# An mLSTM stage reordered: gate columns and decay rows between chunks, key and query pieces in pairs, the head norm in halves

## The chip, the cores and the metric

The kernel runs on one core of one Trainium2 chip. That core has a matrix engine (TensorE, PE in the profile, with its weight loads as PEld), a vector engine (VectorE, DVE), a scalar engine (ScalarE, ACT), a general-purpose engine (GpSimd, POOL), and a queue that issues DMA transfers (SyncE, SP). The engines run at the same time; each takes its own instructions in a fixed order and waits for others through semaphores. The large on-chip memory is SBUF. TensorE writes its results to a second, small memory, PSUM, which has eight banks of 512 float32 values per partition.

The metric is the device time of one execution in microseconds (us), lower being better.

## The reference

A decoder trunk of two layers works on 256 tokens of width 1024, in float32. Each layer is a half-step SwiGLU feed-forward, a token mixing, and another half-step feed-forward, each followed by a residual and a layer norm. The token mixer of layer 1 is the mLSTM, beside a cross-attention of 4 heads into 256 memory tokens; both read one input projection and go into one output projection. What matters here:

```python
def mlstm_mixer(u, b_gates, qk_conv_w, head_norm_g):
    b, s, _ = u.shape
    qk, v, o_pre, gates = jnp.split(u, [2 * D_TOK, 3 * D_TOK, 4 * D_TOK], -1)
    qk = jax.nn.silu(causal_dwconv(qk, qk_conv_w))
    q, k = jnp.split(qk, 2, -1)
    gates = gates.astype(jnp.float32) + b_gates.astype(jnp.float32)
    log_i = gates[..., :ML_HEADS]
    log_f = jax.nn.log_sigmoid(gates[..., ML_HEADS:])
    h = mlstm_chunkwise(q, k, v, log_i, log_f)
    mu = jnp.mean(h, -1, keepdims=True)
    var = jnp.mean(jnp.square(h - mu), -1, keepdims=True)
    h = (h - mu) * lax.rsqrt(var + LN_EPS) * head_norm_g.astype(jnp.float32)
    return jax.nn.sigmoid(o_pre) * h.reshape(b, s, D_TOK).astype(u.dtype)
```

There are 4 mLSTM heads of 192 columns (768 together). The reference steps through chunks of 64 tokens; the kernel computes the same as one masked product over all 256 tokens: scores of queries and keys, weighted by a decay that comes from running sums and maxima of the gates, times the values, divided by the larger of a denominator and an exponential. The convolution is causal over 4 positions, per channel.

## The kernel before

**Precision.** A float32 operand is split into two parts, a rounded one and the rest (`split`, L98: a copy on ScalarE at L99, a difference on VectorE at L100). A product is three products of parts. Where the weights are the stationary operand (`mmw`, L179), the activation's two parts lie side by side, 512 wide: L181 multiplies both by the weight's first part, L182 the first 256 by its second, and `comb` (L184) adds the bank's two halves, with a copy on ScalarE (L186) and an addition on VectorE (L187). Where the activation is stationary, `mm3` (L171) makes the three products at L175 to L177.

**Weights.** `pieces` lists all weights in the order of use, 1 MB each at most. `trace_piece` loads one into one of 3 raw buffers and splits it into one of 5 buffers; `get` asks for one piece ahead of the one that it hands out. In the mLSTM stage two of the raw buffers are lent out: one to the head norm's gains, one to the decay weights.

**Order.** The program is written in Python in a wished order, with pools of buffers; a scheduler then fixes each engine's order, and may put later work that it takes to be ready ahead of earlier work that it takes to wait. Banks of PSUM come from two pools of four, `y` (`ybank`) and `mm` (`mbank`).

**The mLSTM stage** (`mlstm_mixer`, L540), for layer 1: the output gate and the gates (L545 to L564); the query of the cross-attention (`Xattn`, tile `xq`); `gate_rows` (L574), a chain over ScalarE, VectorE and GpSimd on 4 rows, one per head; the values of heads 0 and 1 (`values(0, t)`, L697) and the cross-attention's scores (L429) in turn; `columns` (L603), which turns the gate rows into columns; `decay` (L612) twice, for two heads each, which share one bank; then six pieces of keys and queries (`qk_piece`, L627): keys 0, 1, 2 and then queries 0, 1, 2, each 256 columns in two chunks of 128, with the cross-attention's `values` (L455) between the first ones. A piece's chunk has a bank of its own; `comb` copies it to SBUF, where the convolution reads it, a scaled copy on ScalarE (L637) and three multiply-adds on VectorE (L639), and a Silu on ScalarE ends the piece (L643).

Then come the values of heads 2 and 3, with the scores of all four heads (`mscores`, L648) between them, then `numer` (L661) for the two tiles of 128 tokens: products of scores and values (L673), the division, and the norm of four heads, whose reciprocal root runs on GpSimd (`rstd_of`, L202). `tokens` (L708) multiplies by the gate (L712), transposes (L715) and splits the result into the operand `mix`. `OutProj` (L477) multiplies by the output weights in four quarters `q` of the contraction (tile `yo`): `head` does quarter 0 for both tiles, `rest` the others tile by tile, with quarter 1 of both column halves first; after each half of the columns comes the layer norm's first part (`ln_half`, L211). Tile 0's norm and transposes end under tile 1's products; the next feed-forward begins with products of tile 0 (tile `gx`).

`OutProj` and `Xattn` serve the convolution mixer of layer 0 as well.

## Time and profile before

| | |
|---|---|
| median of 3 runs | 1000.24 us (1000.14 to 1000.39) |
| span of the profiled execution, first to last instruction | 1004.1 us |
| TensorE busy, whole span | 986.8 us (98%) |
| VectorE busy, whole span | 664.8 us (66%) |
| ScalarE busy, whole span | 530.1 us (53%) |
| GpSimd busy, whole span | 39.4 us (4%) |
| TensorE busy from 704.00 to 782.65 us (query to the last head's product) | 77.87 of 78.65 us, mean granted clock 0.91 |
| TensorE busy from 782.65 to 809.60 us (output projection) | 24.98 of 26.95 us, clock 1.00 |

The profiled execution's own time is known as its span alone; it is 3.9 us longer than the median of the runs. Times in the profile count from its first instruction. A row of a stretch has its start and end, its length, the busy time of each engine with the number of instructions, the granted share of TensorE's clock, the mean busy share of the DMA engines and their GB/s. A row of the order in time has start, duration, engine, line, operation, what it writes and reads, and in square brackets how long the engine had been idle and what ended that.

### The profile page before, as it was taken

To read this page: it belongs to the slowest core of one execution; us is meant where nothing else is said; L and a number is where in the kernel's file an instruction comes from. 1 tells how busy PE (TensorE), PEld (TensorE's weight loads), DVE (VectorE), ACT (ScalarE), POOL (GpSimd) and SP (SyncE) were. 2 spreads that over 40 slices of the span, in tenths; PEclk is the share of its full clock that TensorE was granted. 3 is DMA by queue.
4 is the path that set the end of the run, shared out by engine and by line. 5 is a ranking of instruction groups with operands and counts; after the bars stand their busy time and mean duration, and the time that the engine had idled before them with its cause. 6 is when DMAs were issued, how large, how long until landed. Compare 5 with 4: busy or idle time off the path is not lost.

```text
span 1004.1 us, 12980 instructions
## 1 busy us (share of the span) xinstructions
PE 986.8 (98%) x5116; PEld 834.7 (83%) x5116; DVE 664.8 (66%) x1010; ACT 530.1 (53%) x851; POOL 39.4 (4%) x52
## 2 busy tenths in 40 slices
PE   8999999999999999999999999999999999999996
PEld 7888888888888888888788888889788788888885
DVE  6685657868677656565866656576478887556555
ACT  6565555447445545556355555535676346454540
POOL 0000000100000000000100000002300110000001
PEclk9999999999999999999999999999799999999999
DMA  8884546455535654644464646434145466546421
GB/s 277 311 295 166 210 168 212 171 228 205 187 130 187 241 201 159 218 155 180 173 246 168 215 162 213 154 111 154 78 149 205 185 236 230 199 158 216 161 84 43
DMA packets 29293, 186.90 MB, mean 186 GB/s; under 512 B 3632, under 2 KB 4656, under 8 KB 8368
## 3 DMA queue, kind: packets, MB, share of 16 engines
q1 hardware_dynamic: 29232, 186.07, 51.7%
q8 instruction: 40, 0.66, 0.2%
q14 instruction: 21, 0.17, 0.1%
HBM read 185.01 MB, written 1.05 MB: 185 GB/s over the span
## 4 chain that ended last, share of the span: by engine, by line
PE 89%; DVE 4%; POOL 2%; DMA 2%; issue 2%; ACT 0%; SPq 0%; POOLq 0%; DVEq 0%; ACTq 0%
PE gu L181 28%; PE gu L182 14%; PE y L177 8%; PE y L175 8%; PE y L176 8%; PE qkp L181 3%; PE gx L175 2%; PE gx L177 2%; PE gx L176 2%; DVE wl L100 1%; PE qkp L182 1%; PE cx L181 1%; PE cg L181 1%; PE cb L181 1%; PE yo L177 1%
## 5 line engine op out<-in xcount | busy, mean ns | idle before, releaser
L100 DVE TENSOR_TENSOR wl<-raw,wh 128x1024 fp32r<-128x1024 f32 (+1 forms) x342 | 400.6, 1195 | 147.6 <-ACT wh L99 146.8
L181 PE MATMUL gu<-x,wh 128*128 128x512 f32 x1216 | 431.1, 399 | 1.4 <-DVE s L187 1.1
L99 ACT ACTIVATE wh<-raw 128x1024 fp32r<-128x1024 f32 (+1 forms) x342 | 338.3, 1032 | 113.4 <-PE y L177 45.0
L182 PE MATMUL gu<-x,wl 128*128 128x256 f32 x1216 | 340.8, 281 | 0.4 <-DVE wl L100 0.2
L181 PEld LDWEIGHTS gu<-x,wh 128*128 128x128 f32 x1216 | 228.5, 188 | 57.4 <-DVE s L187 1.4
L182 PEld LDWEIGHTS gu<-x,wl 128*128 128x128 f32 x1216 | 230.0, 189 | 2.6 <-DVE wl L100 1.0
L175 PE MATMUL y<-wh,h 128*128 128x512 f32 x352 | 138.1, 392 | 0.0
L177 PE MATMUL y<-wh,h 128*128 128x512 f32 x352 | 137.7, 391 | 0.0
L176 PE MATMUL y<-wl,h 128*128 128x512 f32 x352 | 137.2, 390 | 0.0
L187 DVE TENSOR_TENSOR s<-s,gu 128x256 f32<-128x256 f32 x152 | 63.2, 417 | 107.6 <-ACT s L186 107.6
L186 ACT ACTIVATE s<-gu 128x256 f32<-128x256 f32 x152 | 57.4, 379 | 111.4 <-PE gu L182 110.7
L177 PEld LDWEIGHTS y<-wh,h 128*128 128x128 f32 x352 | 66.1, 188 | 14.5
L175 PEld LDWEIGHTS y<-wh,h 128*128 128x128 f32 x352 | 66.1, 188 | 14.0
L176 PEld LDWEIGHTS y<-wl,h 128*128 128x128 f32 x352 | 66.1, 188 | 13.0
L301 ACT ACTIVATE h<-s 128x256 fp32r<-128x256 f32 x76 | 31.7, 417 | 68.2 <-DVE s L298 68.0
L297 ACT ACTIVATE s<-s 128x256 f32<-128x256 f32 x76 | 31.6, 416 | 37.0 <-DVE s L187 37.0
L302 DVE TENSOR_TENSOR h<-s,h 128x256 fp32r<-128x256 f32 x76 | 32.0, 421 | 17.9 <-ACT h L301 17.9
L181 PE MATMUL qkp<-x,wh 128*128 128x512 f32 x96 | 38.6, 438 | 0.0
L175 PE MATMUL gx<-wh,x 128*128 128x512 f32 x96 | 38.2, 398 | 0.2 <-DVE x L261 0.2
L177 PE MATMUL gx<-wh,x 128*128 128x512 f32 x96 | 37.5, 391 | 0.0
L176 PE MATMUL gx<-wl,x 128*128 128x512 f32 x96 | 37.4, 390 | 0.0
L260 ACT ACTIVATE x<-xt 128x512 fp32r<-128x512 f32 x20 | 11.4, 596 | 44.2 <-PE xt L239 43.8
(191 smaller groups left out, 996.1 us busy)
## 6 DMA issues: line engine op xcount, KB each, us to landing
raw<-in_wgu SPq DMA_DIRECT2D x83, 1024.0 KB, 4.8
raw<-in_wd SPq DMA_DIRECT2D x43, 1024.0 KB, 4.8
raw<-in_wconv SPq DMA_DIRECT2D x10, 1024.0 KB, 4.8
raw<-in_wout SPq DMA_DIRECT2D x8, 1024.0 KB, 4.8
raw<-in_wm SPq DMA_DIRECT2D x7, 1024.0 KB, 4.7
gb<-in_lngb SPq DMA_DIRECT2D x6, 1024.0 KB, 4.9
raw<-in_wkv SPq DMA_DIRECT2D x4, 1024.0 KB, 4.9
raw<-in_wop SPq DMA_DIRECT2D x4, 776.0 KB, 4.2
```

Of the source, the lines that this page charges most:

```text
L99: act.activation(h, raw, AF.Copy)
L100: dve.tensor_sub(l, raw, h.bitcast(F32))
L175: pe.matmul(o, ah, bh, start=start, stop=False)
L176: pe.matmul(o, ah, bl, start=False, stop=False)
L177: pe.matmul(o, al, bh, start=False, stop=stop)
L181: pe.matmul(bank, w[0], a.rearrange("p c t -> p (c t)"), start=start, stop=False)
L182: pe.matmul(bank[:, :T], w[1], a[:, 0], start=False, stop=stop)
L186: act.activation(o, bank[:, T:], AF.Copy)
L187: dve.tensor_add(o, o, bank[:, :T])
L297: act.activation(t_[:, :256], t_[:, :256], AF.Silu)
L301: act.activation(hh, t_[:, 256:], AF.Copy)
L302: dve.tensor_sub(hT[g][:, 1, fc, :], t_[:, 256:], hh.bitcast(F32))
```

## The change

Layer 1's mLSTM stage is written in another order, and some of its steps are cut differently.

- The pieces of keys and queries come in pairs, key 0, query 0, key 1, query 1, key 2, query 2, and their weights stream in that order.
- `proj_direct` replaces `proj_ws` for them. Both chunks of a piece lie in the two halves of one bank; each step of the contraction is three 256-wide products into the same place, so that no addition of halves is needed. The convolution reads PSUM directly. Between the two chunks a function `mid` may put other work: `gate_rows` between the chunks of the cross-attention's query, `columns`, `decay(2)`, the cross-attention's transposes (`turn`) and values, one head of `mscores`, and one `numer`.
- `qk_piece` returns its Silu, which the caller places: those of key 0 and query 0 stand after the second `decay`.
- `Xattn.values` is cut in two; `turn` has all transposes and copies.
- `numer(t, a)` does one pair of heads, with a norm and a reciprocal root of its own, and the multiplication by the gate. Heads 0 and 1 of both tiles come before and within the last query piece; `tokens(t, h)` likewise does one half.
- `OutProj.head(q)` can be called for quarter 1 as well; `rest` does the quarters that are left, half by half of the columns. In layer 0 quarter 1 is thus no longer done ahead for both halves.

Comments and docstrings are dropped, which changes nothing.

```diff
-    order = [("wm", 0), ("wv", 0, 0), ("wv", 0, 1)] + [("wm", i) for i in range(1, 7)]
+    order = [("wm", 0), ("wv", 0, 0), ("wv", 0, 1)] + [("wm", i) for i in (1, 4, 2, 5, 3, 6)]
...
+    def proj_direct(w, name, use, mid=None):
+
+        b = mbank(name)
         for c in range(2):
+            if c and mid:
+                mid()
+            o = b[:, c * T:(c + 1) * T]
+            for k in range(KC):
+                s = slice(k * 256 + c * P, k * 256 + (c + 1) * P)
+                a = cur["x"][:, k]
+                pe.matmul(o, w[0][:, s], a[:, 0], start=k == 0, stop=False)
+                pe.matmul(o, w[0][:, s], a[:, 1], start=False, stop=False)
+                pe.matmul(o, w[1][:, s], a[:, 0], start=False, stop=k == KC - 1)
+            use(c, o)
...
-        def values(self, c):
-            ob = ybank(f"xo{self.l}_{c}")
+        def turn(self, c):
             for e in range(2):
                 n = f"{self.l}_{c}{e}"
-                p = self.p.pop((c, e))
+                p = self.p[c, e]
...
-        def head(self):
-            self.ws[0] = get("wo", self.l, 0)
+        def head(self, q=0):
+            self.ws[q] = get("wo", self.l, q)
             for t in range(2):
-                self.part(0, t, (0, 1))
+                self.part(q, t, (0, 1))
 
         def rest(self, gb):
-            for q in range(1, 4):
+            first = len(self.ws)
+            for q in range(first, 4):
                 self.ws[q] = get("wo", self.l, q)
             nx = new_act(f"x{self.i}")
 
             def tail(t):
-                self.part(1, t, (0, 1))
                 for h in range(2):
-                    for q in range(2, 4):
+                    for q in range(first, 4):
                         self.part(q, t, (h,))
...
-        def qk_piece(n):
-            which = 1 if n < 3 else 0
-            i = n % 3
-            r = tmp(f"qr{n}")
-            ut = tmp(f"qu{n}")
+        def qk_piece(which, i, mid=None):
+            r = tmp(f"qr{which}{i}")
 
             def use(c, b):
                 o = c * 256
-                comb(ut[:, o:o + 256], b)
                 w = [qcw[:, 6 * which + 2 * i + c, q:q + 1] for q in range(4)]
-                act.activation(r[:, o:o + 256], ut[:, o:o + 256], AF.Copy, scale=w[3])
+                act.activation(r[:, o:o + 256], b, AF.Copy, scale=w[3])
                 for q, sh in ((0, 3), (1, 2), (2, 1)):
-                    dve.scalar_tensor_tensor(r[:, o + sh:o + 256], ut[:, o:o + 256 - sh], w[q],
+                    dve.scalar_tensor_tensor(r[:, o + sh:o + 256], b[:, :256 - sh], w[q],
                                              r[:, o + sh:o + 256], op0=ALU.mult, op1=ALU.add)
...
-        xa = Xattn(1, get("wm", 0), mix)
-        gate_rows()
+        xa = Xattn(1, get("wm", 0), mix, gate_rows)
         values(0, 0)
         xa.scores(0)
         values(0, 1)
         xa.scores(1)
-        columns()
+        silu = [qk_piece(1, 0, columns)]
         decay(0)
-        decay(2)
-        qk_piece(0)
-        xa.values(0)
-        qk_piece(1)
+        silu.append(qk_piece(0, 0, lambda: decay(2)))
+        for f_ in silu:
+            f_()
+        qk_piece(1, 1, lambda: xa.turn(0))()
+        mscores(0)
+        qk_piece(0, 1, lambda: xa.values(0))()
+        xa.turn(1)
+        qk_piece(1, 2, lambda: mscores(1))()
         xa.values(1)
-        qk_piece(2)
-        qk_piece(3)
-        qk_piece(4)
-        qk_piece(5)
+        numer(0, 0)
+        qk_piece(0, 2, lambda: numer(1, 0))()
         values(1, 0)
-        mscores(0)
-        mscores(1)
-        values(1, 1)
         mscores(2)
         mscores(3)
-        numer(0)
-        numer(1)
+        values(1, 1)
+        tokens(0, 0)
+        numer(0, 1)
+        numer(1, 1)
+        tokens(1, 0)
         o = OutProj(1, mix, i)
-        tokens(0)
-        o.head()
-        tokens(1)
+        o.head(0)
+        tokens(0, 1)
+        o.head(1)
+        tokens(1, 1)
         o.rest(load_ln(i))
```

More of the change, by code (lines that the diff above doesn't have):

```diff
@@ L402, in mem_kv, with proj_ws @@
                 act.activation(kvs[l][1][:, c], b[:, l * 256:(l + 1) * 256], AF.Copy)
-    def proj_ws(w, name, use):
+    def proj_direct(w, name, use, mid=None):
+        b = mbank(name)
         for c in range(2):
+            if c and mid:
[8 more added lines that the diff above has]
+            use(c, o)
+    def proj_ws(w, name, use, mid=None):
+        for c in range(2):
+            if c and mid:
+                mid()
             b = mbank(f"{name}_{c}")
@@ L416, in trunk, with __init__ @@
     class Xattn:
-        def __init__(self, l, w, mix):
+        def __init__(self, l, w, mix, mid=None):
             self.l, self.mix = l, mix
@@ L465, in values @@
                 act.activation(p, tb, AF.Copy)
+        def values(self, c):
+            ob = ybank(f"xo{self.l}_{c}")
+            for e in range(2):
+                p = self.p.pop((c, e))
                 h0 = (2 * c + e) * 64
@@ new lines, in mlstm_mixer, with numer @@
+        hts = {}
+        def numer(t, a):
+            if a == 0:
+                hts[t] = zp.tile([P, DTOK], F32, tag="z", name=f"ht{t}")
+            ht = hts[t]
+            n = f"{t}{a}"
+            r = sp.tile([P, 2], F32, tag="dn", name="dn" + n)
+            st = sp.tile([P, 2, 6], F32, tag="hst", name="hst" + n)
+            mv = sp.tile([P, 2, 2], F32, tag="hmv", name="hmv" + n)
+            b = mbank("num" + n)
+            bv = b[:, :386].rearrange("p (a e) -> p a e", a=2)
+            for c in range(2):
+                h = 2 * a + c
+                for s in range(t + 1):
+                    lhs = E[h][:, 256:384] if s == 1 else E[h][:, tsl(t)]
+                    pe.matmul(bv[:, c, :], lhs, v1[s][:, h, :], start=s == 0, stop=s == t)
+            dve.tensor_copy(r, bv[:, :, DH])
+            dve.scalar_tensor_tensor(r, r, -1.0, r, op0=ALU.mult, op1=ALU.max)
+            dve.tensor_tensor(r, r, ecol[:, t, 2 * a:2 * a + 2], op=ALU.max)
+            dve.reciprocal(r, r)
+            dve.tensor_tensor(ht[:, 384 * a:384 * a + 384].rearrange("p (a e) -> p a e", a=2),
+                              bv[:, :, :DH], r[:, :, None].to_broadcast([P, 2, DH]), op=ALU.mult)
+            for c in range(2):
+                h = 2 * a + c
+                dve.bn_stats(st[:, c, :], ht[:, DH * h:DH * h + DH])
+                dve.bn_aggr(mv[:, c, :], st[:, c, :])
+            rs = rstd_of(mv[:, :, 1], 2, "hn" + n)
+            for c in range(2):
+                s = slice(DH * (2 * a + c), DH * (2 * a + c) + DH)
+                dve.tensor_scalar(ht[:, s], ht[:, s], mv[:, c, 0:1], rs[:, c:c + 1],
@@ L706, in values, with tokens @@
                            AF.Copy)
-        def tokens(t):
-            og = ogs[t]
-            for h in range(2):
-                s = slice(384 * h, 384 * h + 384)
-                dve.tensor_mul(og[:, s], og[:, s], hn[t][:, s])
-                b = mbank(f"tk{t}{h}")
-                for c in range(3):
-                    pe.transpose(b[:, c * P:(c + 1) * P], og[:, (3 * h + c) * P:(3 * h + c + 1) * P],
-                                 ident)
-                to_parts(mix, 3 * h, 3, t, b)
-        xa = Xattn(1, get("wm", 0), mix)
-        gate_rows()
+        def tokens(t, h):
+            b = mbank(f"tk{t}{h}")
+            for c in range(3):
+                pe.transpose(b[:, c * P:(c + 1) * P], ogs[t][:, (3 * h + c) * P:(3 * h + c + 1) * P],
+                             ident)
+            to_parts(mix, 3 * h, 3, t, b)
+        xa = Xattn(1, get("wm", 0), mix, gate_rows)
         values(0, 0)
@@ L771, in scores, with values @@
         xa.scores(1)
-    conv_mixer(mix, [scores, lambda: xa.values(0), lambda: xa.values(1)])
+    def values(c):
+        xa.turn(c)
+        xa.values(c)
+    conv_mixer(mix, [scores, lambda: values(0), lambda: values(1)])
     o = OutProj(0, mix, 1)
```

37 lines of the change are left out of this document (5 added, 32 removed).

## The prediction

> **What bounds the kernel now.** I read the page for the span, a table of stretches for the stage that the change touches, the order of single instructions on TensorE (PE) around each loss, and the groups of the pieces.
>
> ```profile
> span 1004.1 us, 12980 instructions
> PE 986.8 (98%) x5116; PEld 834.7 (83%) x5116; DVE 664.8 (66%) x1010; ACT 530.1 (53%) x851; POOL 39.4 (4%) x52
> ```
>
> TensorE is busy for 98% of the span, so time can only come from work removed there, from its idle stretches, or from its clock. The stretches (us, then busy time of each engine, then the granted clock):
>
> ```profile
> core 0: us, PE busy (x) PEld busy (x) DVE busy (x) ACT busy (x) POOL busy (x), PEclk, DMA share, GB/s
> 713.69:717.10 3.41, 2.63 (x16) 1.59 (x15) 3.09 (x9) 2.42 (x9) 1.95 (x3) 1.00 0.00 0
> 717.34:730.99 13.65, 13.65 (x38) 9.57 (x37) 8.69 (x24) 8.04 (x25) 0.00 (x0) 0.50 0.00 0
> 731.00:767.50 36.50, 36.50 (x219) 31.76 (x219) 31.04 (x59) 27.98 (x48) 0.00 (x0) 1.00 0.49 163
> 704.00:782.65 78.65, 77.87 (x407) 64.10 (x405) 55.52 (x115) 52.28 (x100) 7.72 (x10) 0.91 0.38 134
> 782.65:809.60 26.95, 24.98 (x118) 19.91 (x118) 24.13 (x59) 9.58 (x13) 6.47 (x6) 1.00 0.60 230
> ```
>
> Three losses stand there. The second row is the largest: TensorE is busy throughout 13.65 us, but with half its clock. The row above is the stretch before: 3.41 - 2.63 = 0.78 us idle, and much of the busy time on narrow operands. The last row, the output projection, has 26.95 - 24.98 = 1.97 us idle. The pieces after 731 us run with no idle time at all.
>
> What TensorE did around the drop, and how far a step of a piece is from the next, before and after the clock came back:
>
> ```profile
> 713.82 0.70 PE L434 MATMUL sc<-kT,xqT 64*128 64x256 f32 x2
> 714.97 1.13 PE L434 MATMUL sc<-kT,xqT 64*128 64x256 f32 x6 [0.45 <-ACT p L446]
> 716.02 0.22 PE L606 MATMUL cols<-ident,rows 4*128 4x4 f32 x1
> 716.58 0.22 PE L607 MATMUL cols<-ident,rows 4*128 4x4 f32 x1 [0.34 <-POOL rows L598]
> ...
> 716.79 1.52 PE L616 MATMUL negm<-rows,ident 4*128 4x256 f32 x4
> ...
> 719.05 0.63 PE L181 MATMUL qkp<-x,wh 128*128 128x512 f32 x1
> 719.69 0.63 PE L181 MATMUL qkp<-x,wh 128*128 128x512 f32 x1
> ...
> 723.02 1.22 PE L616 MATMUL negm<-rows,ident 4*128 4x256 f32 x2
> ...
> 735.94 0.40 PE L181 MATMUL qkp<-x,wh 128*128 128x512 f32 x1
> 736.18 0.28 PE L182 MATMUL qkp<-x,wl 128*128 128x256 f32 x1
> 736.30 0.40 PE L181 MATMUL qkp<-x,wh 128*128 128x512 f32 x1
> ```
>
> The last scores, the gate columns and the decay rows use 64 or 4 rows of the array and wait for ScalarE (ACT) and GpSimd (POOL); right after them the clock is halved. A step of a piece then takes 719.69 - 719.05 = 0.64 us instead of 736.30 - 735.94 = 0.36.
>
> **The change, part by part.** *Clock.* Both chunks of the first key piece, dense work, now stand on either side of the columns, and the next piece's on either side of the second decay pair. No stretch as long as that of 713.69 to 717.10 is left with narrow work and waits alone. What this is worth: at least the first piece's 2 x 8 steps, 16 x 0.28 = 4.5 us; at most half of the stretch, 6.8 us. The stretch also holds decay matmuls, slowed as well, so I take a value near the top, 6.3.
>
> [...]
>
> *Idle time before the columns.* The GpSimd chain ends only just before 716.58; with a chunk of a piece ahead of the columns they are done in time. Of the 0.78 us I take all, bounds 0 and 0.8, since the dense chunk (8 x 0.36 = 2.9 us) is longer than both waits.
>
> *The pieces themselves.* A step was a 512-wide and a 256-wide matmul; it becomes three 256-wide ones into one place of the bank, the same 768 columns. The row at 736.18 is a 256-wide one, and the next starts 0.12 us later with its weights loaded: 3 x 0.12 = 0.36, as now. Cost nothing; bounds -0.01 and +0.02 a step, 96 steps, so -1 to +2 us. What goes is the addition of the bank's halves:
>
> ```profile
> L100 DVE TENSOR_TENSOR wl<-raw,wh 128x1024 fp32r<-128x1024 f32 x12 | 14.6, 1219 | 1.8 <-ACT wh L99 1.7
> L99 ACT ACTIVATE wh<-raw 128x1024 fp32r<-128x1024 f32 x12 | 12.6, 1057 | 0.6 <-DMA raw<-in_wm 0.6
> L637 ACT ACTIVATE qr<-qu,qcw 128x256 f32<-128x256 f32 x11 | 5.6, 505 | 0.7 <-DVE qu L187 0.6
> ...
> L639 DVE SCALAR_TENSOR_TENSOR qr<-qu,qcw,qr 128x253 f32<-128x253 f32 x11 | 5.2, 477 | 2.3 <-ACT qr L637 2.3
> ...
> L187 DVE TENSOR_TENSOR qu<-qu,qkp 128x256 f32<-128x256 f32 x11 | 4.5, 414 | 1.2 <-ACT qu L186 1.2
> L186 ACT ACTIVATE qu<-qkp 128x256 f32<-128x256 f32 x11 | 4.2, 380 | 6.6 <-PE qkp L182 6.6
> ```
>
> Twelve times 0.38 us leave ScalarE and 0.41 us leave VectorE (DVE): 4.6 and 5.0 us, none of it on TensorE's path, which had no idle time there. I count it at zero; it makes room for half of the head norms, which move under the pieces.
>
> *The shared bank.* Both chunks of a piece now lie in one bank, which the convolution reads in place. Whether TensorE may write the second chunk while the first is read is shown by the decay bank, also shared by two heads: the pair at 723.02 starts after the first head's last read, and both heads' matmuls are issued in the program one after the other.
>
> ```profile
> 720.53 0.37 ACT L622 ACTIVATE decays<-negm,cols 128x128 f32<-128x128 f32 x1
> ```
>
> The first four decay matmuls are so few because they belong to one head of each bank; the second heads come later. So each piece gets a new wait: chunk 0's end, one L637 (0.50), three L639 (1.43), handovers of some 0.3, together 2.3 us when the queues are empty; up to 2.3 + 1.06 + 1.22 = 4.6 when a weight split stands ahead on both engines. Behind the waiting matmul stands all of TensorE's queue, and behind that the scores. In the trace such a wait was filled: seven steps of a piece stand before the pair at 723.02, and TensorE was busy throughout. The next piece's first chunk (2.9 us) plus the work put between the chunks is longer than 2.3, shorter than 4.6 at times. Bounds 0 and 12 (the second is the rival below); I take 2.0, some 0.3 us a piece.
>
> *Head norm split in four, two of them early.* The output projection's idle time:
>
> ```profile
> 789.13 0.52 PE L715 MATMUL tk<-ident,og 128*128 128x128 f32 x3 [0.89 <-DVE og L712]
> 790.23 0.50 PE L175 MATMUL yo<-wh,mix 128*128 128x512 f32 x1 [0.35 <-DVE og L712]
> ...
> 797.72 0.99 PE L715 MATMUL tk<-ident,og 128*128 128x128 f32 x6 [0.73 <-DVE og L712]
> ...
> 784.31 1.25 POOL L204 TENSOR_SCALAR hn0v<-hmv 128x4 f32<-128x4 f32 x1 [67.79 <-DVE dn L675]
> 785.65 1.05 POOL L206 TENSOR_TENSOR hn0r<-hn0v,mhalf 128x4 f32<-128x4 f32 x1
> ```
>
> 0.89 + 0.35 + 0.73 = 1.97 us, the whole idle time of the stage, end with the gated heads. With heads 0 and 1 done before, the projection's quarters 0 and 1 (2 x 24 matmuls of 0.23 us, 11.0 us) lie over two half chains. Saved 2.0, bounds 0 and 2.0. The two extra pairs on GpSimd (2.3 us each) are off the path, as it has idle time in plenty; but VectorE waits for them in its queue, 1.3 us at worst per half, under pieces.
>
> *What is late next.* Quarter 1 of tile 1 was done after tile 0's; now it stands before. So tile 0's layer norm has only 24 matmuls of the projection over it, not 36.
>
> ```profile
> 800.03 1.49 DVE L217 SCALAR_TENSOR_TENSOR z<-xnat,yo 128x512 f32<-128x512 f32 x2
> 801.43 1.28 DVE L218 BATCH_NORM_STATS2 st<-z 128x6 f32<-128x512 f32 x2
> 802.63 1.21 DVE L100 TENSOR_TENSOR wl<-raw,wh 128x1024 fp32r<-128x1024 f32 x1
> ...
> 808.48 0.69 DVE L261 TENSOR_TENSOR x<-xt,x 128x512 fp32r<-128x512 f32 x1 [0.18 <-ACT x L260]
> ...
> 809.48 0.39 PE L177 MATMUL yo<-wh,mix 128*128 128x512 f32 x1
> 809.71 0.40 PE L175 MATMUL gx<-wh,x 128*128 128x512 f32 x1
> ```
>
> From 800.03 to the first half of the new activation, 809.17, are 9.1 us; the next product starts at 809.71. The cover becomes 24 x 0.23 + 0.9 (transposes) = 6.4 us. If the first half's L217 and L218 are done early, as the order now allows, and one weight split is not in the way, the chain is 9.1 - 1.4 - 1.2 = 6.5. Bounds 0 and 2.7 us; I take 1.0, nearer to the short chain.
>
> *Layer 0* gets its transposes grouped and its quarter 1 spread over the two halves of the columns; the work is the same. Zero, with bounds of one wait of the kind above, 0.9 us, on either side.
>
> **Sum.** Removed 6.3 + 0.8 + 2.0 = 9.1; added 2.0 + 1.0 = 3.0; net 6.1 us less. The profiled execution's span of 1004.1 us would become 998.0. It lies 3.9 us above the median of the runs, 1000.24, and I carry the difference over as it is: **994.1 us**.
>
> **Rivals.** *The clock is not won* (B). The drop may come at another place, since columns and decay rows remain narrow, or the runs without the profile may not have it: their three times agree within 0.25 us, and the profiled one is 3.9 us longer. Against it stands how clearly the drop follows the narrow stretch. Without 6.3 us the net is +0.2: 1000.4. A form of it is a drop in the runs that is only as long as the stretch ahead of it, 3.41 us: half of that, 1.7 us, is then won in place of 6.3, the net is -1.5, and the time 998.7.
>
> *The waits on the bank are not filled* (C), on the other side. TensorE's order is fixed ahead; where it puts a piece's second chunk behind no more than the work between the chunks, each piece stands still. The middle of the chain is 3.45 us; the longest work between is one head of scores, half of this row:
>
> ```profile
> 775.31 3.73 PE L654 MATMUL ms<-qk 128*128 128x256 f32 x16
> ```
>
> So a stop is 3.45 - 1.87 = 1.6 us at least and about 2.5 where little is between: 6 x 2.05 = 12.3, against 9.1 won, plus 1.0: +4.2, 1004.4 us. It turns slower once the stops exceed 8.1 us, 1.35 a piece. For it speaks that the bank has no second copy; against it the filled wait at 723.02. [...]
>
> *VectorE becomes the bound of the pieces* (D): it was busy 31.04 of 36.50 us there, loses 4.5 us of additions in that stretch, and gets two half norms with their waits for GpSimd. Also, if the order lets a Silu in ahead of the last Exp, two table loads come on ScalarE:
>
> ```profile
> 737.95 1.28 ACT L643 ACT_TABLE_LOAD   x1 [1.05 <-DVE qr L639]
> ```
>
> With 2.6 us on ScalarE's part of the chain and 0.5 on VectorE, the net is 6.1 - 3.1 = 3.0: 997.2.
>
> **Chances.** Forecast 0.55 (its own range 991 to 997.5: 4.5 to 6.8 on the clock, 0.5 to 5 added); B 0.20 (0.05 of it for the short drop); C 0.13; D 0.12. About 0.2%, 2 us, is what a measurement of this kernel can tell from no change. Faster: forecast 0.54, B 0.05, D 0.10, together 0.69. Slower: B 0.04, C 0.11, D 0.01, together 0.16. Same: 0.15. The range reaches down to 990 (everything won, waits nearly all filled) and up to 1001.5, which takes in B and leaves most of C out.
>
> **What would show it.** Right: the clock row at 1.00 throughout the stage; L181 gone from the pieces; no L186 and L187 there; idle time of TensorE ahead of second chunks under 0.5 us each; no wait of tk for L712; the first gx waiting about 1 us for the new activation. Wrong: a second stretch at half clock; idle time "<-DVE qr L639" on TensorE of more than 1 us in each piece; more than one table load between 716 us and the projection; the projection's stage longer than 26.95 us.

## The result, and the profile after

The changed kernel takes **1012.24 us** (median of 4 runs, 1009.03 to 1012.50), the kernel before 1000.32 beside it: ratio 1.0102, 95% interval 1.0083 to 1.0122. It is slower; 994.1 was predicted, and the range ended at 1001.5.

The profiled execution of the kernel before, on which the prediction rests, was itself an unusual one: with some 2 us outside its span it took about 1006 us, where the median of the kernel's runs is 1000. A second profile of the same kernel (first experiment) is an ordinary execution, and "before" means that one from here on. The profile after is of the fastest of the four runs, 1009.03 us with a mean clock of 0.993; the others, 1012.05 to 1012.50, have 0.990 and 0.991, so part of what they lose to half clock stands in no trace. The first parts of the pages, before and after:

```profile
span 998.3 us, 12980 instructions
PE 981.8 (98%) x5116; PEld 831.9 (83%) x5116; DVE 664.6 (67%) x1010; ACT 530.4 (53%) x851; POOL 39.4 (4%) x52
```

```profile
span 1006.9 us, 13162 instructions
PE 987.3 (98%) x5212; PEld 839.2 (83%) x5212; DVE 661.4 (66%) x998; ACT 529.2 (53%) x841; POOL 38.9 (4%) x56
```

TensorE is as full as it was; it is busy for longer. The stretches tell where (start:end, length, busy time of TensorE, its weight loads, VectorE, ScalarE and GpSimd, then the granted clock). Before: the gate columns and decays, the half clock within them, the pieces, the output projection.

```profile
715.50:724.10 8.60, 8.21 (x33) 5.84 (x33) 6.53 (x23) 7.34 (x25) 0.00 (x0) 0.83 0.00 0
724.10:761.20 37.10, 37.10 (x222) 32.25 (x221) 32.66 (x60) 28.70 (x49) 0.00 (x0) 0.99 0.46 160
776.80:803.80 27.00, 25.02 (x118) 19.96 (x118) 24.18 (x59) 9.66 (x13) 6.47 (x6) 1.00 0.61 230
721.20:724.65 3.45, 3.45 (x12) 2.87 (x12) 2.71 (x7) 3.45 (x8) 0.00 (x0) 0.51 0.00 0
```

After: the pieces, the stop ahead of the last scores, and the half clock that follows.

```profile
715.90:767.90 52.00, 50.66 (x360) 43.78 (x359) 37.21 (x80) 34.36 (x62) 1.84 (x2) 1.00 0.38 132
767.90:774.20 6.30, 3.69 (x23) 3.35 (x21) 6.06 (x17) 3.98 (x6) 0.51 (x2) 0.97 0.45 166
773.80:784.05 10.25, 9.85 (x28) 7.45 (x29) 3.51 (x7) 0.63 (x2) 0.75 (x2) 0.50 0.30 103
```

In this execution the half clock around 717 us is gone, and the pieces run at full clock. But 10.25 us at half clock stand at 773.80, behind a stop: 6.30 - 3.69 = 2.6 us idle. What TensorE, VectorE and ScalarE did there, after the change:

```profile
770.67 0.59 PE L671 MATMUL ms<-qk 128*128 128x256 f32 x2
771.10 0.49 PE L731 MATMUL tk<-ident,og 128*128 128x128 f32 x3
774.21 1.94 PE L671 MATMUL ms<-qk 64*128 64x256 f32 x4 [2.61 <-ACT qk L660]
```

```profile
768.25 1.22 DVE L100 TENSOR_TENSOR wl<-raw,wh 128x1024 fp32r<-128x1024 f32 x1
769.39 0.55 DVE L709 TENSOR_TENSOR og<-og,ht 128x384 f32<-128x384 f32 x1
...
769.93 1.22 DVE L100 TENSOR_TENSOR wl<-raw,wh 128x1024 fp32r<-128x1024 f32 x1
...
771.14 0.46 DVE L656 SCALAR_TENSOR_TENSOR qr<-qkp,qcw,qr 128x253 f32<-128x253 f32 x1
771.52 0.55 DVE L697 TENSOR_TENSOR ht<-num,dn 128x384 f32<-128x384 f32 x1
771.98 0.47 DVE L656 SCALAR_TENSOR_TENSOR qr<-qkp,qcw,qr 128x254 f32<-128x254 f32 x1
772.37 0.61 DVE L701 BATCH_NORM_STATS2 hst<-ht 128x6 f32<-128x192 f32 x2
...
772.98 0.45 DVE L656 SCALAR_TENSOR_TENSOR qr<-qkp,qcw,qr 128x255 f32<-128x255 f32 x1
```

```profile
767.98 1.06 ACT L99 ACTIVATE wh<-raw 128x1024 fp32r<-128x1024 f32 x1 [2.64 <-PE qkp L415]
768.94 0.46 ACT L654 ACTIVATE qr<-qkp,qcw 128x256 f32<-128x256 f32 x1
...
773.52 0.63 ACT L660 ACTIVATE qk<-qr 128x512 f32<-128x512 f32 x1 [1.40 <-DVE hmv L702]
```

The last query chunk is done at about 768. Its convolution waits behind a weight split on ScalarE, then behind two weight splits and the early head norm (L709, L697, L701) on VectorE; the Silu ends at 774.15, and the scores that need it are next in TensorE's queue. Before, 12 us of work stood between that chunk, which ended at 757.5, and these scores: `values(1, 0)`, the scores of heads 0 and 1 (the first row below) and `values(1, 1)`, some 4.2, 3.5 and 4.2 us. The second row has the scores that need the chunk:

```profile
761.71 3.73 PE L654 MATMUL ms<-qk 128*128 128x256 f32 x16
...
769.44 3.73 PE L654 MATMUL ms<-qk 128*128 128x256 f32 x16
```

In the changed order heads 0 and 1 are done earlier, `values(1, 1)` is written behind the scores, and the scheduler put 8 of the 24 matmuls of `values(1, 0)` ahead of the chunk. What is left lasts, with two scores and three transposes, from 767.9 to 771.6.

A second stop is at the cross-attention's last scores. After the change, TensorE and VectorE:

```profile
710.63 0.70 PE L451 MATMUL sc<-kT,xqT 64*128 64x256 f32 x2
713.39 1.13 PE L451 MATMUL sc<-kT,xqT 64*128 64x256 f32 x6 [2.07 <-ACT p L463]
```

```profile
709.51 0.68 DVE L615 TENSOR_TENSOR_SCAN rows<-rows 4x256 f32<-4x256 f32 x1 [5.51 <-POOL rows L613]
711.02 0.68 DVE L617 TENSOR_TENSOR_SCAN rows<-rows 4x256 f32<-4x256 f32 x1 [0.83 <-POOL rows L616]
711.63 1.25 DVE L458 TENSOR_REDUCE nm<-sc 128x2 f32<-128x512 f32 x2
```

`gate_rows` now stands between the query's chunks. Its scans wait for GpSimd, and the softmax's maximum (L458) is queued behind them. The exponential (L463), for which TensorE waits here, needs that maximum: 2.07 us where the kernel before lost 0.45.

### The profile page after: what moved, and what is told of

The parts are those of the page before. It is cut to its first block, busy times and chain, and to the rows that moved or that the text cites. A ratio compares the mean times of both kernels' runs of the same rounds, so it can differ in the third digit from the quotient of the medians.

```text
span 1006.9 us, 13162 instructions
## 1 busy us (share of the span) xinstructions
PE 987.3 (98%) x5212; PEld 839.2 (83%) x5212; DVE 661.4 (66%) x998; ACT 529.2 (53%) x841; POOL 38.9 (4%) x56
## 4 chain that ended last, share of the span: by engine, by line
PE 89%; DVE 3%; ACT 2%; DMA 2%; POOL 1%; issue 1%; SPq 0%; POOLq 0%; DVEq 0%; ACTq 0%
PE gu L181 28%; PE gu L182 14%; PE y L177 8%; PE y L175 8%; PE y L176 8%; PE gx L177 2%; PE gx L176 2%; PE gx L175 2%; PE cx L181 1%; PE cg L181 1%; PE cb L181 1%; PE xt L239 1%; PE ms L671 1%; PE qkp L414 1%; ACT wh L99 1%; PE yo L177 1%
## 5 line engine op out<-in xcount | busy, mean ns | idle before, releaser
L298 DVE SCALAR_TENSOR_TENSOR s<-s 128x256 f32<-128x256 f32 x76 | 32.1, 422 | 1.2
```

The lines of the kernel that those rows point to most:

```text
L298: dve.scalar_tensor_tensor(t_[:, 256:], t_[:, :256], 0.5, t_[:, 256:], op0=ALU.mult, op1=ALU.mult)
```

## Where the time went

From the two traces I added up, from the cross-attention's query to the first product of the next feed-forward, the time from each TensorE instruction's start to the next one's, by result tile. It is 107.58 us before and 118.01 after. Half clock accounts for 10.24 - 3.41 = 6.83 us at half speed, at most 3.4 us of time. The other 7.0:

| | us |
|---|---|
| stop ahead of the last mLSTM scores (ms) | +2.61 |
| stop at the cross-attention's scores (sc), 0.45 to 2.07 | +1.62 |
| idle within the pieces | +0.66 |
| wait of the transposed weights (pT) for the decays | +0.55 |
| wait of the new activation's transposes (xt) | +0.20 |
| waits of tk and yo for the gated heads, 1.99 to 0.64 | -1.35 |
| waits of the columns and decays | -0.60 |
| 96 steps of 0.360 us in place of 0.347 | +1.25 |
| the rest, all of it busy time (xo 3.18 for 2.14, among others) | +2.1 |

Most of the rest fits the places where TensorE changes from one tile to another: 55 times in place of 37 in this stretch. The first matmul of a piece behind such a change takes 0.22 us to the next (742.12 to 742.34, after the change), and the others 0.12:

```profile
740.13 2.06 PE L671 MATMUL ms<-qk 128*128 128x256 f32 x8
742.12 0.39 PE L416 MATMUL qkp<-x,wl 128*128 128x256 f32 x1
742.34 0.28 PE L414 MATMUL qkp<-x,wh 128*128 128x256 f32 x1
742.46 0.28 PE L415 MATMUL qkp<-x,wh 128*128 128x256 f32 x1
```

At full clock the pieces have some 1.2 us more busy time than their steps explain, and xo, cut into 4 runs instead of 2, has 1.0. No run changed this alone.

Each run is listed with the mean granted clock of its span, so all runs can be split in the same way: time x clock is taken as the time at full clock, time x (1 - clock) as what half clock cost. The split is rough. The trace that the prediction used and the one after the change have 3.5 and 4.4 us at half clock at the program's end (from 1000.64 and 1002.48), 1.7 and 2.2 us of the last column, and the clock is recorded to three digits, some 0.5 us. Means over the runs; each ratio is to runs of the kernel before that were taken beside it, with medians of 999.64 (1 to 4), 999.92 (5 to 8), 1000.22 (9 to 12) and 1000.41 us (13 to 15). Kernel N is the one of experiment N.

| kernel | median us | ratio to before (95%) | at full clock | lost to half clock |
|---|---|---|---|---|
| before (15 runs beside the first set) | 999.64 | | 995.9 | 3.9 |
| changed | 1012.24 | 1.0102 (1.0083 to 1.0122) | 1002.7 | 8.9 |
| 1 before, again | 999.66 | | 995.4 | 4.2 |
| 2 values ahead of the scores | 1004.50 | 1.0040 (1.0026 to 1.0053) | 1000.4 | 3.7 |
| 3 norm late | 1010.55 | 1.0106 (1.0087 to 1.0124) | 1000.6 | 10.1 |
| 4 own banks | 1007.21 | 1.0069 (1.0054 to 1.0084) | 1002.0 | 5.0 |
| 5 tail alone | 1003.50 | 1.0034 (1.0021 to 1.0047) | 997.2 | 6.4 |
| 6 gate rows late | 1003.62 | 1.0035 (1.0022 to 1.0048) | 999.5 | 4.3 |
| 7 values first, own banks | 1004.46 | 1.0037 (1.0024 to 1.0051) | 999.3 | 5.0 |
| 8 columns between, alone | 1003.79 | 1.0030 (1.0019 to 1.0042) | 998.2 | 5.3 |
| 9 tail with cover | 1003.47 | 1.0036 (1.0023 to 1.0049) | 998.1 | 5.8 |
| 10 stop filled | 1007.92 | 1.0073 (1.0057 to 1.0089) | 1004.6 | 3.4 |
| 11 values first, cover | 1007.28 | 1.0068 (1.0046 to 1.0089) | 1001.7 | 5.7 |
| 12 steps alone | 1002.14 | 1.0020 (1.0006 to 1.0033) | 998.1 | 4.7 |
| 13 wide decays | 999.14 | 0.9979 (0.9968 to 0.9991) | 996.5 | 2.8 |
| 14 columns filled | 1001.51 | 1.0006 (0.9991 to 1.0020) | 998.4 | 3.3 |
| 15 columns between, wide decays | 1001.36 | 0.9999 (0.9987 to 1.0011) | 997.7 | 3.3 |

## The experiments

**1. The kernel before, once more.** No edit.

> The kernel before, once more, for its clock. Theory A: the 13.65 us at half clock around 717 us belong to the one profiled execution, and the runs do not have them (their times lie about 6 us under that execution's): this profile has the clock at 1.00 through the stage and a span of about 998 us. Theory B: the drop is in every execution, and the profile alone makes it longer: a span of about 1004 us again, with a drop.

The profiled execution has one half-clock stretch of 3.41 us in the stage, at 721.20, and a span of 998.3 us. The 13.65 us of the profile that the prediction used belong to that execution.

**2. Values ahead of the scores.** In the changed kernel:

```diff
         values(1, 0)
+        values(1, 1)
         mscores(2)
         mscores(3)
-        values(1, 1)
```

> The changed kernel with values(1,1) ahead of mscores(2) and mscores(3). Theory S (one stop at the end of the pieces): TensorE stood still for 2.8 us at 771 us, since the scores wait for the last query's convolution and Silu and nothing stands in between, and the stop brings the half clock. 4.2 us of value products in that place fill the stop, so about 2.8 us and the half clock (5 to 8 us) go: 1001 to 1004 us, clock 1.00 from 768 us on. Theory W (many small waits on the shared banks and 256-wide steps): the time stays at 1009 us or more, for the stop is only one of them.

1004.50: 7.7 us less than the changed kernel. In the profile the scores run without a wait, at full clock:

```profile
777.27 3.73 PE L671 MATMUL ms<-qk 128*128 128x256 f32 x16
```

The stop and the half clock behind it are thus two thirds of the loss.

**3. The norm late**, so that VectorE is free for the last convolution. In the changed kernel:

```diff
-        numer(0, 0)
-        qk_piece(0, 2, lambda: numer(1, 0))()
+        qk_piece(0, 2)()
...
         values(1, 1)
+        numer(0, 0)
+        numer(1, 0)
```

> The changed kernel with the half norms of heads 0 and 1 (numer(0,0), numer(1,0)) behind the value products, not under the last query piece. Theory S in the form that VectorE's queue makes the last convolution late: 6 us of VectorE work leave the place ahead of it, the stop shrinks from 2.8 us to under 1 us, and with it the half clock: 1002 to 1006 us. If the shared bank alone makes the last piece late, the stop stays over 2 us and the time at 1009 us or more.

1010.55. The stop ahead of the scores is 1.49 us, not gone: two weight splits, 2.4 us, still stand in VectorE's queue ahead of and between the convolution's steps. The profiled execution spends 17.0 us of the stage at half clock, in three stretches (6.8 us from 715.70, 3.4 from 732.70 and 6.8 from 780.50). So the early norm makes the stop longer, but the stop does not depend on it.

**4. A bank for each chunk**, with the addition of halves, as before. In the changed kernel:

```diff
+                comb(ut[:, o:o + 256], b)
...
-            proj_direct(get("wm", (1 if which else 4) + i), f"qkp{which}{i}", use, mid)
+            proj_ws(get("wm", (1 if which else 4) + i), f"qkp{which}{i}", use, mid)
```

> The changed kernel with a bank for each chunk and the addition of halves, as before, in the new order. Theory W: no second chunk waits, steps take 0.352 us again: the loss goes, 1000 to 1004 us. Theory S: VectorE gets 5 us of additions back, the last convolution is as late or later, the stop at the scores stays 2 us or more, and the time at 1008 us or more.

1007.21. The idle time within the pieces is 0.89 us (0.66 with the shared bank), so the shared bank did not hold the pieces up. The stop ahead of the scores remains, with 1.82 us, yet no half clock follows in the profile: 5.0 us are lost to it in the mean where the changed kernel loses 8.9. Why a stop of 1.8 us is followed by half clock in kernel 2 (1.79 us, 13 to 15) and not here, this run does not show.

**5. The tail alone.** The kernel before, with the head norm, tokens and quarters 0 and 1 in halves (`numer(t, a)`, `tokens(t, h)`, `head(q)` as in the change; `numer(0, 0)` and `numer(1, 0)` behind `values(1, 1)`).

> The kernel before with one part of the change alone: the head norm in halves, tokens in halves, head(0) and head(1), with the halves of heads 0 and 1 behind the last value products. Theory: this part is a gain by itself; the waits of the transposes tk for the gated heads (1.6 us) go and nothing takes their place: 1.2 to 1.6 us less, 998.1 to 998.5 us against 999.7. Rival: VectorE's queue or the shorter cover over tile 0's layer norm takes it back: 999.5 us or more, with idle time ahead of xt or gx.

1003.50: this part of the change alone costs time. The order of TensorE where tile 0's new activation is due, in this run:

```profile
803.36 1.29 PE L239 MATMUL xt<-ident,xnat 128*128 128x128 f32 x8 [1.35 <-DVE xnat L229]
805.89 0.79 PE L175 MATMUL gx<-wh,x 128*128 128x512 f32 x1 [1.24 <-ACT x L260]
```

Two waits, 2.6 us, and then half clock for 6.8 us (0.50 from 805.00 to 811.80; the matmul at 805.89 takes 0.79 us). Only 24 products of tile 1 stand over tile 0's layer norm. The waits for the gated heads, which the halves were to remove, are still 1.35 us in three places.

**6. The gate rows behind the whole query**, in kernel 2:

```diff
-        xa = Xattn(1, get("wm", 0), mix, gate_rows)
+        xa = Xattn(1, get("wm", 0), mix)
+        gate_rows()
```

> e1_values_first with gate_rows behind the cross-attention's query, as before, not between its chunks. Theory: the earlier gate chain put both running-sum scans ahead of the scores' maxima in VectorE's queue, where they wait for GpSimd; TensorE's idle time in the scores (1.8 us against 0.45 before) comes from that. With the chain late it falls to about 0.5 us and the time to 1003 us or a little under (from 1004.5). Rival: the scores wait for banks that something else holds: idle time and time as in e1.

1003.62. The scores run without a wait (8 in one row at 710.93), but the columns wait 0.82 us for GpSimd and the pieces 1.27 us more for the decays: the gate chain is as long as it was, and is waited for one step later. The intervals of 2 and 6 overlap; no gain is shown.

**7. Kernel 2 with a bank for each chunk**, the edits of 2 and 4 together.

> e1_values_first with a bank for each chunk, 512-wide steps and the addition of halves. Theory: three 256-wide matmuls of 0.120 us in place of 0.230 + 0.117 cost 96 x 0.013 = 1.2 us, and with the waits on the shared bank some 2 us go: 1002.3 to 1003.3 us. Rival: VectorE's 5 us of additions bring back the stop ahead of the scores, as in e3: 1005 us or more.

1004.46, no change against 1004.50. With the wider steps and the additions the time at full clock is 1.1 us less, which is within what half clock varies by.

**8. The columns between the chunks, alone.** In the kernel before:

```diff
-        columns()
+        silu = qk_piece(0, columns)
         decay(0)
         decay(2)
-        qk_piece(0)
+        silu()
```

> The kernel before with columns between the chunks of the first key piece, and that piece's Silu behind both decays; nothing else. Theory of the prediction: with dense work ahead of columns the stretch at half clock (3.4 us in an ordinary execution, 1.7 us lost) and the waits for GpSimd (0.34 us) and in the decay rows (0.39 us) go: 997.3 to 998.0 us. Rival: the drop follows the waits inside the scores, which stay: a stretch at half clock as before, 999.2 to 999.8 us.

1003.79: the first half of the step from which the prediction's largest term came makes the kernel slower (the second half, the next piece on either side of the second decay pair, was not run alone). The columns' wait is longer (0.92 for 0.34), and the narrow decays now stand together with the transposed weights. The half clock of this run:

```profile
723.97:730.80 6.83, 6.69 (x17) 4.17 (x18) 1.81 (x6) 6.50 (x15) 0.00 (x0) 0.50 0.00 0
```

The half clock has moved by 3 us and doubled.

**9. The tail with its cover.** Kernel 5, with quarter 1 of tile 1 written behind tile 0:

```diff
+                if t and first == 2:
+                    self.part(1, 1, (0, 1))
...
-        o.head(1)
+        o.head(1, (0,))
```

> The kernel before with the head norm and the tokens in halves (as in the run of the tail alone), but quarter 1 of tile 1 of the output projection stays behind tile 0, under tile 0's layer norm, as in the kernel before. Theory L (the tail alone was slower because tile 0's layer norm had 12 matmuls, 2.8 us, less over it): the waits of xt (1.51) and of the first gx (1.41) go, and with them the half-clock stretch of 6.8 us that began at 805 us (price up to 3.4): from 1003.5 down to 999.0 to 1000.3, level with the kernel before. Rival M (the smaller pieces of the norm, twice the tiny operations on GpSimd, cost by themselves): it stays above 1002.

1003.47, no change. The scheduler brought most of that quarter forward again: 28 products stand over tile 0's norm, not 36. With those 4 products more, 0.9 us, the two waits are 1.45 + 0.55 = 2.0 us in place of 2.6. So the waits go with the cover, but the edit did not restore it, and the half clock behind them stayed (the matmuls from 807.67 to 809.80 take 0.63 us each).

**10. The stop filled.** In the changed kernel the last query chunk's matmuls are issued once more into a bank that nobody reads (24 of 256 columns, not needed by the result).

```diff
+            if (which, i) == (0, 2):
+                fb = mbank("fill")
+                for k in range(KC):
...
+                        pe.matmul(fb[:, :T], w[ww][:, s], a[:, p], start=k == 0 and m == 0,
+                                  stop=k == KC - 1 and m == 2)
```

> The changed kernel with the matmuls of the last query piece's second chunk issued once more into a bank that nobody reads: 24 more matmuls of 0.12 us, 2.9 us of TensorE work that the result does not need. About half of them come to stand between the last query chunk and the scores, so that the stop of 2.6 us ahead of the scores is filled. Theory K (the stop is what halves the clock for 10.2 us, and that half clock, 5.1 us, is the larger part of the loss): work is added and the time still falls, 1012.2 + 2.9 - 2.6 - 5.1 = 1007.4, range 1005.5 to 1009; no half clock between 770 and 790 us. Rival (the clock falls for another reason, such as the narrow rows around 715 us or chance): 1012 to 1013.

1007.92, as Theory K expected (1007.4). With 3 us of useless work added, the kernel is 4.3 us faster. The stretch around the scores in this run:

```profile
766.00:790.00 24.00, 24.00 (x149) 21.82 (x149) 19.47 (x47) 11.18 (x16) 3.66 (x4) 1.00 0.46 167
```

No idle time, full clock. Over all runs the added work shows as 1.9 us more at full clock, and 5.5 us less are lost to half clock.

**11. Values first, quarter 1 behind tile 0.** Kernel 2 with the edit of 9.

> The changed kernel with both v products ahead of the last scores (as in the run of 1004.5 us), and quarter 1 of tile 1 of the output projection back behind tile 0. Theory L: the xt wait (0.7) goes and what the shorter cover cost, at most 1.4 us, is won: 1003 to 1004. Rival (the cover is no longer short here because heads 0 and 1 are done early): 1004.5, no change. Both expect it to stay above the kernel before, 1000, because the 256-wide steps (+1.25) and the stop in the decays' part (1.8) remain.

1007.28, 2.8 us more, against both expectations. Here the scheduler kept all 36 products behind tile 0, but in both kernels it put xt behind the first 17 of them, and xt waits 0.66 us as in kernel 2 (0.68). Without that quarter ahead of them the tokens wait for the gated heads, 1.70 us in one place: 12 products cannot cover both.

**12. The steps alone.** The kernel before with three 256-wide matmuls a step, a bank per chunk, the convolution reading the bank:

```diff
-                comb(ut[:, o:o + 256], b)
...
-            proj_ws(get("wm", 1 + n), f"qkp{n}", use)
+            proj_direct(get("wm", 1 + n), f"qkp{n}", use)
```

> The kernel before, where only the q and k pieces are changed: three matmuls of 256 columns a step instead of one of 512 and one of 256, and the convolution reads the bank in place, a bank of its own for each chunk, without the addition of two halves. Theory (a step costs 0.360 instead of 0.347 us, and the additions lay off the path): 96 x 0.013 = +1.25 us, 1001.2. Rival (the additions were worth something: the last query piece is done 0.8 us earlier, and VectorE is less full): 998.5 to 999.8.

1002.14, as the theory expected within its interval (+0.6 to +3.3 us). Matmuls of this run, 0.12 us apart, three to a step; then those of the kernel before, two to a step:

```profile
740.15 0.28 PE L411 MATMUL qkp<-x,wh 128*128 128x256 f32 x1
740.27 0.28 PE L412 MATMUL qkp<-x,wl 128*128 128x256 f32 x1
740.39 0.28 PE L410 MATMUL qkp<-x,wh 128*128 128x256 f32 x1
```

```profile
740.22 0.39 PE L181 MATMUL qkp<-x,wh 128*128 128x512 f32 x1
740.45 0.28 PE L182 MATMUL qkp<-x,wl 128*128 128x256 f32 x1
740.56 0.39 PE L181 MATMUL qkp<-x,wh 128*128 128x512 f32 x1
```

0.36 us against 0.34 to 0.35. No gain from the additions that go, 9.6 us on ScalarE and VectorE, shows in the time.

**13 to 15. Narrow rows and the half clock.** In the trace that the prediction used the clock changes at 717.34, 730.99 and 1000.64 us, 13.65 and 269.65 us apart, which is 4 and 79 times 3.413; in the one after the change at 773.79, 784.03 and 1002.48, 10.24 and 218.45 apart, 3 and 64 times. The shortest stretch is that of the ordinary execution, 3.41 us. So I took the traces in windows of 3.41 us, counted from where a half-clock stretch begins, and added up TensorE's busy time, once as it is and once with each matmul weighted by the share of 128 rows that its form uses ("64*128" is 64 rows). The weight is a way of counting, my estimate of what matters; 13 and 15 try it. Windows ahead of a stretch, and three ahead of none:

| kernel | window | busy us | weighted by rows | half clock behind it, us |
|---|---|---|---|---|
| before, the prediction's profile | 713.92:717.34 | 2.63 | 0.86 | 13.65 |
| 2 | 711.39:714.80 | 1.62 | 1.02 | some 3.4 |
| changed | 770.40:773.80 | 1.19 | 1.19 | 10.24 |
| 13 | 711.30:714.72 | 2.63 | 1.27 | 3.41 |
| 8 | 720.56:723.97 | 2.18 | 1.34 | 6.83 |
| 3 | 777.10:780.50 | 1.91 | 1.38 | 6.8 |
| 7 | 710.60:714.00 | 1.73 | 1.38 | some 6.8 |
| 9 | 803.60:807.00 | 1.45 | 1.45 | at least 3 |
| 5 | 801.60:805.00 | 1.67 | 1.67 | 6.8 |
| before, 1 | 714.38:717.79 | 3.08 | 1.78 | none |
| before, 1 | 717.80:721.20 | 3.01 | 1.81 | 3.41 |
| changed | 712.35:715.76 | 2.37 | 1.84 | none |
| changed | 708.94:712.35 | 2.38 | 2.04 | none |

Busy time without the weights does not tell the two kinds apart: it is 3.01 us in one window ahead of a stretch and 2.94 in another (kernel 3, 729.30:732.70), and 2.37 in one ahead of none. The ordinary execution of the kernel before has one window of each kind, 1.78 and 1.81, with decays of 4 rows that count for nearly nothing in this sum.

The two executions of the kernel before differ in such windows. In the one that the prediction used, the last scores, the columns and the first decays fell into one window, with 0.86 us by rows. The four windows of the stretch behind it hold 2.53, 2.31, 2.30 (slowed decays and other narrow rows) and 3.41 us, and full clock followed the last; the three after the change hold 1.86, 3.04 and 3.41. In the ordinary execution the windows stood 1.2 us earlier against the scores, and one half-clock window, full at once, was all.

A stop, too, falls into the windows in more than one way. After the change, the two windows over which the stop at the cross-attention's scores (2.07 us) is spread, 2.04 and 1.84 us weighted; then the one window of kernel 2 that holds most of this stop (1.79 us), 1.02 weighted, behind which the clock is halved:

```profile
708.94:712.35 3.41, 2.38 (x13) 1.73 (x11) 2.00 (x4) 0.03 (x1) 1.82 (x3) 1.00 0.01 2
712.35:715.76 3.41, 2.37 (x17) 1.99 (x18) 2.75 (x9) 2.31 (x10) 1.01 (x2) 1.00 0.00 0
```

```profile
711.39:714.80 3.41, 1.62 (x9) 0.95 (x8) 2.34 (x6) 1.58 (x7) 2.07 (x3) 1.00 0.00 0
```

How kernel 4's stop of 1.82 us fell is not shown: the clock is 1.00 from 769.50 to 776.30, so no stretch begins there to count from.

*13.* The kernel before, decays contracted over 128 rows, 124 of them zero:

```diff
+            dve.memset(rows[0][:, 2, :], 0.0)
...
-                pe.matmul(o, ident[:NH, h:h + 1].to_broadcast([NH, P]), e, start=True, stop=True)
+                pe.matmul(o, ident[:, h:h + 1].to_broadcast([P, P]), rows[0][:, 2, :], start=True, stop=True)
```

> The kernel before, where the four decay matmuls contract over 128 rows, 124 of them zero, instead of 4; the order on TensorE is the same instruction by instruction, and VectorE gets one memset of 128x256 (about 0.3 us, off the path). Theory G (the gate weighs a window's busy time by the rows in use): the windows after the scores hold about 1.1 us more each (2.28 us of decay matmuls over two windows), 2.9 in place of 1.8, so no half-clock stretch between 710 and 730 us; the time falls by half of 3.4 to 6.8 us where the drop was, median 997.5 to 999.3 against 1000.2. Rival (rows of zeros do not count, or the waits alone make the drop): a half-clock stretch of 3.4 us or more stays there, 1000.2 within 0.7.

999.14 against 1000.41, ratio 0.9979 (0.9968 to 0.9991): the only kernel here that is faster than the kernel before, by 0.2%. Its time at full clock is the same (996.5 and 996.2); the loss to half clock falls from 4.7 to 2.8 us. The profiled execution is one of the three of 12 at a lower clock, and shows what is left:

```profile
711.30:714.72 3.42, 2.63 (x16) 1.50 (x14) 3.10 (x8) 2.42 (x9) 2.20 (x3) 1.00 0.00 0
714.72:718.13 3.41, 3.41 (x11) 2.86 (x10) 3.36 (x13) 2.23 (x11) 0.00 (x0) 0.50 0.00 0
```

Here the window ahead of the stretch happens to hold all the last scores, of 64 rows, the columns and both waits, and no decays: 1.27 us weighted. The part of the expectation that no stretch would stay was thus too strong.

*14.* The kernel before with six dense 512-wide matmuls, which the result does not need, between the columns and the decays (`pe.matmul(fb, a[:, 0, :P], a...)` in `columns`).

> The kernel before with six 512-column matmuls of the activation with itself, into a bank that nobody reads, between the columns and the decays: 6 x 0.23 = 1.4 us of work that the result does not need. Theory G: the windows there are full enough, no half-clock stretch between 710 and 730 us; +1.4 - 1.7 to -3.4 gives 998.3 to 1000. Rival (the drop comes from the waits ahead of the columns and the narrow rows, whatever stands behind): the stretch stays and the time is 1001.6.

No half clock from 710 to 735 us of the profile (clock 1.00, TensorE busy for 24.13 of 25.00 us), and 3.3 us lost in the mean in place of 4.7. It is not gone from all runs: two of the twelve, 1003.82 and 1006.70 us, have a clock of 0.994 and 0.991. The work added costs more than is won: 1001.51, no better than before. The decays with rows of zeros add no time on TensorE (1.02 us for four, 1.12 with 4 rows; 15).

*15.* Kernel 8 with the wide decays and nothing else changed.

> The run with the columns between the chunks of the first key piece (1003.8 us, half clock for 6.8 us from 724 us), with decay matmuls of 128 rows as above and nothing else changed. Theory G: the window ahead of the drop held 1.34 us by rows, of it 2 decay matmuls (0.6 us) and the turned weights behind waits; it comes to about 1.9, at the edge, so the drop goes in some of the executions: 1001 to 1003, no stretch longer than 3.4 us. Rival: no change, 1003.8, 6.8 us at half clock.

1001.36 in place of 1003.79, and no half clock from 710 to 735 us (clock 1.00), where kernel 8 had 6.83 us. The decays of this run, and of kernel 8:

```profile
719.71 1.02 PE L619 MATMUL negm<-rows,ident 128*128 128x256 f32 x4
...
723.48 1.53 PE L619 MATMUL negm<-rows,ident 128*128 128x256 f32 x4 [0.72 <-ACT decays L625]
```

```profile
720.37 1.12 PE L618 MATMUL negm<-rows,ident 4*128 4x256 f32 x4
...
724.11 2.07 PE L618 MATMUL negm<-rows,ident 4*128 4x256 f32 x4 [0.72 <-ACT decays L624]
```

At full clock four decays take 1.02 us with 128 rows and 1.12 with 4. The wait of 0.72 us and the order are the same, and the clock stays up.

## Why the prediction was wrong

**The clock, 6.3 us.** This term was mis-sized twice. It stood for a stretch that one execution had; in an ordinary one it is 3.41 us long and worth 1.7, as the last form of rival B had it. Carrying the difference of 3.9 us over then took the 6.3 off a median whose runs did not have that stretch; besides, it set a span against times, which are some 2 us longer than their spans, so the execution lay about 5.9 us above the median. And "no stretch as long as that of 713.69 to 717.10 is left with narrow work and waits alone" was true of the place and false of the kernel. Kernel 8 shows that moving the columns by itself only shifts the narrow work, with 6.83 us at half clock behind it in place of 3.41, and in the new order kernels 2, 3, 7 and 10 all drop to half clock at the stop ahead of the cross-attention's scores or right behind it (the clock is 0.50 from 715.70 in 3; the six scores behind the stop take 1.61, 2.07 and 1.31 us in 2, 7 and 10, and 1.13 at full clock); the changed kernel's own profile has none there. What helped was the rows of zeros in the decays (13, 15). Nor did it take much idle time: the windows ahead of the half clock have 0.78 us of it in the execution that the prediction used and 0.40 in the ordinary one.

**Idle time before the columns, 0.8 us.** The columns' own 0.34 us was won, but `gate_rows` moved as well, and its scans put 1.62 us on the scores. The prediction looked at what waits for the gate chain, not at what is queued behind its waits on VectorE.

**The tail, 2.0 us.** 1.35 of it came after the change, since tokens have the projection's quarters over them. **What is late next, 1.0 us**, measured 0.20 there. Apart from the other parts (5) the same steps have neither the gain nor the cover, and lose 3.5 us. The two terms were counted as independent; they compete for the same 12 products (11).

**The shared bank, 2.0 us**: nothing that the trace shows. The 0.66 us of idle time within the pieces are three waits, for the decays (0.20), a weight split (0.27) and the cross-attention's weights (0.19), none for the convolution that reads the bank. Rival C, which ended on the slower side, had the wrong place. **Steps of 256, 0**: +1.25 us, inside its bounds of -1 to +2. **The additions, 0**: nothing speaks against it (12). **Layer 0, zero**: from its query to the next feed-forward 86.6 us against 87.1, within the bounds of 0.9.

**Not in the sum.** This is the step that failed most: the wait of the last scores for the last query piece stood at nothing. The stop there and the half clock behind it are 7.7 us of the 12 (2). The early head norm was put under the pieces at no cost, because TensorE had no idle time there; whether the last piece's convolution would still come in time was not asked, though the order left 3.7 us of work over it in place of 12. Rival D had the right engine, VectorE's queue, and priced it at 0.5 us. Its table loads came as well, three in place of one:

```profile
728.25 1.28 ACT L660 ACT_TABLE_LOAD   x1
...
730.19 1.28 ACT L641 ACT_TABLE_LOAD   x1
...
737.84 1.28 ACT L660 ACT_TABLE_LOAD   x1
```

So the first Silu does not follow all Exp work, although the program writes it behind the second decay: the scheduler lets one in between two decays. What this cost was not run by itself; the one wait behind it that the profile shows for the decays is that of the transposed weights, 0.55 us.

Still open: the 2.1 us of other busy time, whose cause is argued from the changes of tile and not shown, and what sets where the clock's changes lie against the work in an execution.

## What to carry to other kernels

Profile the kernel before twice before a term of the sum rests on a stretch at half clock, and price such a stretch by its ordinary form, here the shortest (3.41 us in place of 13.65). When work is moved earlier under a dense stretch, follow the last operand of that stretch through its engine's queue: the cover behind it is what the move uses up. Where a narrow matmul can be padded with zero rows at the same duration (four decays in 1.02 us, against 1.12), that was the cheapest of the ways tried here to lose less to half clock (2.8 us in place of 4.7).

## What the runs showed of the hardware

The half-clock stretches that the profiles show inside the program are 3.41 us long (the kernel before, 13), 6.83 (8), 10.24 (changed) and 13.65 (the prediction's profile). In the table of 13 to 15 they stand behind windows with 0.86 to 1.81 us of busy time weighted by rows; behind three others, with 1.78, 1.84 and 2.04, the clock stayed up. Four decay matmuls of 4 rows took 1.12 us, and of 128 rows 1.02 (8 and 15); the profile with the 4 rows had 6.83 us at half clock, and the one with rows of zeros none. In the kernel before the same padding brought the mean loss from 4.7 to 2.8 us (13). A stop of 1.79 us was followed by half clock in one kernel's profile (2), and one of 2.07 us not in another's (the changed kernel). The kernel before's own times go with the clock: of its runs beside the last set (999.55 to 1004.60 us), six of the eight above 1002 us have a mean clock of 0.991 to 0.994, all below it 0.995 to 0.997.
